# Matmul with rotary embedding on one core: later quarter loads, sixteen block pairs, a split head and a finer last two quads

## The chip, the cores and the metric

The kernel runs on 1 core of one Trainium2 chip. The metric is device time in microseconds (us). Before the change it was 163.15 us, the median of 3 runs (161.26 to 163.74).

## The reference, cut to what matters

```python
batch, seq, hidden, n_heads = (16, 512, 768, 12)      # float32, head_dim = 64
y = np.matmul(x, weight)                              # (16, 512, 768) x (768, 768)
y = y.reshape(batch, seq, n_heads, head_dim)
y1, y2 = y[..., :32], y[..., 32:]
out1 = y1 * cos1 - y2 * sin1                          # cos, sin: (512, 64), the same for all heads
out2 = y2 * cos2 + y1 * sin2
out = np.concatenate([out1, out2], axis=-1).reshape(batch, seq, hidden)
```

## The kernel before, in words

The 8192 rows of x are cut into 64 tiles of 128 rows. Four tiles that use the same rows of cos and sin (the same `r`, four batches) make a quad; there are 16 quads, g = 0 to 15. A tile's products are 12 matmuls: six chunks of 128 of the contracted 768, each in a piece of 512 and one of 256 columns. A quad fills 3072 columns of PSUM, which is six banks of 512 (`py`); two more banks (`pt`) take transposes.

For the product, x has to be cast to fp16 and turned, so that the contracted index lies on partitions. There are two ways:

- **By TensorE.** SyncE loads the tile whole (`load`, L189, 384 KB, rows of 3072 bytes) into one of 10 buffers `xs`. ScalarE casts it (`cast`, L169, `xc<-xs`), TensorE transposes six blocks of 128 x 128 into a PSUM bank (`turn`, L235, `pt<-ident,xc`), and ScalarE copies them back (`xt<-pt`).
- **As a block pair.** Two tiles are loaded together in four quarters (`load_quarter`, L204), each to 32 partitions in pieces of 192 numbers (768 bytes), in such an order that VectorE's transposes of 32 x 32 blocks are all that is left (`turn_pair`, L260, `xp<-xd` or `xp<-xh`). A pair of kind `sp` is loaded by SyncE as fp32 into `xb` (3 buffers) and cast by ScalarE in one instruction (`cast_pair`, `xd<-xb`). A pair of kind `pool` is loaded by GpSimd's queue, which casts to fp16 on the way (`xh<-in_x_dram`); GpSimd spends its own time on issuing these loads. `BLOCKS` names the pairs: the second half (g, 1) of quads 2 to 14, seven of them `sp` and six `pool`. So 26 tiles go by pairs and 38 by TensorE.

After the product, `rope` (L304, L313) takes 1024 columns at a time (a unit, two banks; `units`): VectorE multiplies them from PSUM by cos and by sin in one instruction (`tq<-py,csn`, 2048 results), and GpSimd adds the two halves, one of them with its 32-column halves swapped, into the output buffer (`ov<-tq`). `tq` has three buffers, `ov` four quads. `store` sends 1536 columns of a quad to HBM, from ScalarE's queue, at the first and third tile of the next quad. The last quad has its own units: five of 512 columns, one of 320, and one of 192 in the bank `pt0`, whose add VectorE does.

The order on each engine is written out by hand. `Flow.do` records every instruction with what it reads and writes, and puts the waits in. SyncE first issues the loads `order = [0, "w0", 1, "w1", 2, "w2", 3, "w3", "w4", "w5"]` (x tiles 0 to 3, six chunks of the weight), then cos and sin, and then `fetch`, a list in which x tiles and quarters take turns, as far as buffers are free (`pump`). Quad 0 is computed chunk by chunk as the weight lands (L407 to L442): 12 matmuls on zeros (`warm`), casts of the weight on VectorE (`cast_w`), the products of each chunk (`mm0`). From tile 4 on a loop (L501 to L525) emits, for tile i: its 12 matmuls, the ropes that they complete, the block transposes for tiles up to i + 5 (`B_AHEAD` 6), TensorE's transposes for tile i + 3 (`T_AHEAD` 3), the cast for tile i + 7 (`C_AHEAD` 7), GpSimd's loads for tiles up to i + 19 (`P_AHEAD` 20), and the stores. At the end SyncE waits for all stores (L529), and the program's own closing steps follow (L560: each engine's drain, barriers, a clearing of semaphores). `tile_critical(no_gpsimd_drain=True)` leaves GpSimd's drain out at the end of the hand-written part, so its first one is in the closing steps.

Of the kernel before, what the change touches and what calls it, by code (L numbers as in the profile page):

```python
# [16 lines left out]
class Flow:  # L17
# [23 lines left out]

    def do(self, e, make, reads=(), writes=(), dma=None, tick=True):
        need = {}
        for k in reads:
            for s, v in self.wrote.get(k, {}).items():
                need[s] = max(need.get(s, 0), v)
        for k in writes:
            for d in (self.wrote, self.readby):
                for s, v in d.get(k, {}).items():
                    need[s] = max(need.get(s, 0), v)  # L50
# [53 lines left out]
def kernel(  # L104
# [10 lines left out]
    nc = tc.nc  # L115
# [15 lines left out]
    CHUNKS = [(t, e) for t in range(NT) for e in range(2)]  # L131
    LAST = NG - 1


    BLOCKS = {}
    for g in range(2, 15):
        BLOCKS[g, 1] = "pool" if g % 2 == 0 and g >= 4 else "sp"

    def sbuf(name, shape, dt):
        return nc.alloc_sbuf_tensor(name, shape, dt).ap()  # L140

    NX, NB, NBH, NC, NCP, NXT, NXP, NTQ, NOV = 10, 3, 3, 5, 2, 8, 4, 3, 4

# [6 lines left out]
    xs_b = [sbuf(f"xs{i}", [P, H], FP32) for i in range(NX)]  # L150
    xb_b = [sbuf(f"xb{i}", [P, 2 * H], FP32) for i in range(NB)]
    xh_b = [sbuf(f"xh{i}", [P, 2 * H], FP16) for i in range(NBH)]
# [40 lines left out]
    def load_quarter(gh, q):  # L193
        g, h = gh
        b, r = where(g * QB + 2 * h)
        e = BLOCKS[gh]
        src = x[b : b + 2].rearrange("b (j a r) (q k) -> r q a (b j) k", r=SB, a=R, q=NQ)
        if q == 0:
            xs[gh] = ring("xh", NBH) if e == "pool" else ring("xb", NB)
        k = xs[gh]  # L200
        name = f"xh{k}" if e == "pool" else f"xb{k}"
        buf = xh_b[k] if e == "pool" else xb_b[k]
        dst = buf.rearrange("p (j k) -> p j k", j=2 * NQ)
        do(e, lambda eng: eng.dma_start(out=dst[ts(q, R)], in_=src[r, q]),  # L204
           writes=[f"{name}q{q}"], dma=name)

# [6 lines left out]

    def cast_w(c, e):
        t, h = c
        do(e, copy(e, w_sb[:, t, h], w_raw[:, t, h]),
           reads=[f"wr{t}{h}"], writes=[f"w{t}{h}"])


    def cast(i, e):  # L220
        k = xs[i]
        c = ring("xc", NC)
        xc[i] = c
        do(e, copy(e, xc_b[c].rearrange("p (t m e) -> p t m e", t=NT, e=2),
                   xs_b[k].rearrange("p (m t e) -> p t m e", t=NT, e=2)),
           reads=[f"xs{k}"], writes=[f"xc{c}"])

    def turn(i, e):
        c = xc[i]
        k = ring("pt", 2)  # L230
        z = ring("xt", NXT)
        src = xc_b[c].rearrange("p (t m e) -> p t e m", t=NT, e=2)
        pt = pt_b[k].bitcast(FP16)[:, 0:H].rearrange("p (t e m) -> p t e m", t=NT, e=2)
        for t, h in CHUNKS:
            do("pe", lambda eng: eng.transpose(pt[:, t, h, :], src[:, t, h, :], ident),  # L235
               reads=[f"xc{c}", "ident"], writes=[f"pt{k}"], tick=(t, h) == CHUNKS[-1])
        do(e, copy(e, xt_b[z], pt), reads=[f"pt{k}"], writes=[f"xt{z}"])
        xT[i] = (lambda t, h: xt_b[z][:, t, h, :], f"xt{z}")

# [8 lines left out]
    def turn_pair(gh):  # L248
# [12 lines left out]
        for s in (0, 1):  # L261
            xT[g * QB + 2 * h + s] = (
                lambda t, e, s=s: v[:, t, e, ts(s, P)], f"xp{z}")

    def units(g):
        if g < LAST:
            return [(c, c + 1024, py[:, c : c + 1024], [f"ps{c // 512}", f"ps{c // 512 + 1}"], "pool")
                    for c in (0, 1024, 2048)]  # L270
        u = [(c, c + 512, py[:, c : c + 512], [f"ps{c // 512}"], "pool") for c in range(0, 2560, 512)]
        u.append((2560, 2880, py[:, 2560:2880], ["ps5"], "pool"))
        u.append((2880, 3072, pt_b[0][:, 0:192], ["pt0"], "dve"))
        return u

    def pieces(g, s):

        out_, lo = [], s * H
        for c0, c1, ps, banks, _ in units(g):
            step = 512 if len(banks) > 1 else c1 - c0  # L280
            for k, b in enumerate(banks):
                a, z = max(lo, c0 + k * step), min(lo + H, c0 + (k + 1) * step)
                if a < z:
                    out_.append((a, z, ps[:, a - c0 : z - c0], b))
        return out_

    def mm_piece(i, piece, c, start, stop, tick):
        g, s = divmod(i, QB)
        a, z, ps, bank = piece
        get, key = xT[i]  # L290
        t, h = c
        do("pe", lambda eng: eng.matmul(  # L292
            ps, get(t, h), w_sb[:, t, h, a - s * H : z - s * H], start=start, stop=stop),
            reads=[key, f"w{t}{h}"], writes=[bank], tick=tick)

    ov_of = {}

    def rope(g, u):
        c0, c1, ps, banks, adder = u
        w, r = c1 - c0, g % SB  # L300
        k = ring("tq", NTQ)
        nh = w // D
        tq = tq_b[k][:, :, 0:w]
        do("dve", lambda eng: eng.tensor_tensor(  # L304
            out=tq.rearrange("p j (h d) -> p j h d", d=D),
            in0=ps.rearrange("p (h d) -> p h d", d=D)
            .unsqueeze(1).broadcast_to((P, 2, nh, D)),
            in1=csn[:, :, r, :].unsqueeze(2).broadcast_to((P, 2, nh, D)),
            op=MULT), reads=banks + ["csn"], writes=[f"tq{k}"])
        if g not in ov_of:  # L310
            ov_of[g] = ring("ov", NOV)
        o = ov_of[g]
        do(adder, lambda eng: eng.tensor_tensor(  # L313
            out=ov_b[o][:, ds(c0, w)].rearrange("p (h t d) -> p h t d", t=2, d=HD),
            in0=tq[:, 0].rearrange("p (h t d) -> p h t d", t=2, d=HD),
            in1=tq[:, 1].rearrange("p (h t d) -> p h t d", t=2, d=HD)[:, :, ::-1, :],
            op=ADD), reads=[f"tq{k}"], writes=[f"ov{o}c{c}" for c in range(c0, c1, 64)])

# [19 lines left out]

    order = [0, "w0", 1, "w1", 2, "w2", 3, "w3", "w4", "w5"]
    for k in order:  # L340
# [9 lines left out]

    fetch, quarters = [], []
    soon = [p for p in sorted(BLOCKS) if BLOCKS[p] == "sp"]
    for i in range(QB, NTILE):
        if soon and i >= (soon[0][0] - 1) * QB:
            quarters += [(soon[0], q) for q in (0, 2, 1, 3)]
            soon.pop(0)
        if not is_block(i):
            fetch.append(i)
            if quarters:
                fetch.append(quarters.pop(0))  # L360
        elif quarters and quarters[0][0] == pair_of(i):
            fetch.append(quarters.pop(0))
    fetched = [0]
    xs_used, xb_used = [0], [0]
    xs_sent, xb_sent = [4], [0]

# [35 lines left out]

    def castx(i, e):
        cast(i, e)
        xs_used[0] += 1

    U0 = units(0)  # L407
    warm(9)
    castx(0, "dve")
    cast_w(CHUNKS[0], "dve")  # L410
    turn(0, "dve")
    castx(1, "act")
    warm(3)
    mm0(0, CHUNKS[0])
    cast_w(CHUNKS[1], "dve")
    turn(1, "act")
    mm0(0, CHUNKS[1])
    mm0(1, CHUNKS[0])
    mm0(1, CHUNKS[1])
    castx(2, "act")  # L420
    cast_w(CHUNKS[2], "dve")
    turn(2, "act")
    for i in (0, 1):
        mm0(i, CHUNKS[2])
    castx(3, "act")
    for c in CHUNKS[:3]:
        mm0(2, c)
    turn(3, "act")
    cast_w(CHUNKS[3], "dve")
    for i in (0, 1, 2):  # L430
        mm0(i, CHUNKS[3])
    for c in CHUNKS[:4]:
        mm0(3, c)
    cast_w(CHUNKS[4], "dve")
    for i in range(4):
        mm0(i, CHUNKS[4])
    cast_w(CHUNKS[5], "dve")
    do("dve", lambda eng: eng.tensor_copy(
# [3 lines left out]
        reads=["sin", "csn1", "cos"], writes=["csn"])  # L442
    assert not quarters
    pump()

    state = {"cast": 4, "turn": 4, "bturn": 0, "pool": 0}
    pairs = sorted(BLOCKS)
    pool_pairs = [p for p in pairs if BLOCKS[p] == "pool"]

    def casts(upto):  # L450
        while state["cast"] < min(upto, NTILE):
            i = state["cast"]
            state["cast"] += 1
            if not is_block(i):
                castx(i, "act")
            elif i % 2 == 0 and BLOCKS[pair_of(i)] == "sp":
                cast_pair(pair_of(i))
                xb_used[0] += 1
            pump()

    def turns(upto):
        while state["turn"] < min(upto, NTILE):
            i = state["turn"]
            state["turn"] += 1
            if not is_block(i):
                turn(i, "act")

# [16 lines left out]

    C_AHEAD, T_AHEAD, B_AHEAD, P_AHEAD = 7, 3, 6, 20


    for i in range(4):
        mm0(i, CHUNKS[5])
        if i == 1:  # L490
            casts(6)
            turns(5)
            rope(0, U0[0])
    casts(7)
    turns(6)
    rope(0, U0[1])
    rope(0, U0[2])
    casts(8)
    turns(7)

    for i in range(QB, NTILE):  # L501
# [12 lines left out]
        turns(i + 1 + T_AHEAD)  # L514
        casts(i + 1 + C_AHEAD)
        pool_loads(i + P_AHEAD)
# [9 lines left out]
    store(LAST, 2 * H, 3 * H, "sp")  # L526
    store(LAST, 3 * H, 2880, "act")
    store(LAST, 2880, 4 * H, "sp")
    f.finish("sp", [f"ov{o}c{c}" for o in range(NOV) for c in range(0, QB * H, 64)])  # L529
# [35 lines left out]
```

## Time and profile before

| | |
|---|---|
| median of 3 runs | 163.15 us (161.26, 163.15, 163.74) |
| the profiled execution | 162.36 us, span 160.6 us |
| busy share | PE 91%, DVE 80%, POOL 79%, ACT 45% |
| mean granted TensorE clock | 0.974 |
| DMA | 50.77 MB, mean 316 GB/s |
| HBM | 27.79 MB read, 25.17 MB written |

PE is TensorE's matmuls, PEld its weight loads, DVE is VectorE, ACT ScalarE, POOL GpSimd, SP SyncE; a q behind a name is the engine's sequencer, which waits, branches and issues DMAs. L292 is line 292 of the kernel. A group row gives the line, the engine, the operation, what is written and read, the count, then the busy time and the mean of one in ns, and behind the bar the idle time of the engine just before, with what ended it. The chain of waits is followed back from the last instruction: at each step to what released it. Times in a timeline are from the span's start. The span is what the profiler saw on the core; the device time of the same execution is 1.8 us more.

### The profile page before, as it was taken

What the parts mean: (1) busy time and instruction counts of PE and PEld (TensorE: products, weight loads), DVE (VectorE), ACT (ScalarE), POOL (GpSimd) and SP (SyncE); (2) the same over time, 40 slices, a digit from 0 to 9 for tenths busy, and PEclk for the clock granted to TensorE, in tenths of its full rate; (3) what the DMA queues carried; (4) which work ended last, traced back from release to release, by engine and by line L of the source; (5) the groups of instructions that cost most, each with busy time, mean ns of one, the idle gap of its engine ahead of it and who ended that gap; (6) DMA issues with size and microseconds to landing.
All of it is one profiled execution on the core that took longest, in us unless ns stands there. A gap on an engine that the chain in (4) does not pass through costs nothing.

```text
span 160.6 us, 2527 instructions
## 1 busy us (share of the span) xinstructions
PE 145.8 (91%) x1014; PEld 90.0 (56%) x1014; DVE 128.1 (80%) x77; ACT 72.2 (45%) x82; POOL 127.2 (79%) x81
## 2 busy tenths in 40 slices
PE   6889569999999999999999999999999999999600
PEld 2336336656565666666666666665656566666500
DVE  0624783499999799989999899897989899789830
ACT  3272466895234653454354527461655247131000
POOL 1000299749999999999999998999989797988950
PEclk9999987999999999999999999999999999999985
DMA  4999999999999999999999999999999975555860
GB/s 107 409 406 319 259 265 278 275 330 356 347 335 354 367 396 280 353 382 400 296 351 388 410 302 354 377 411 316 351 372 404 416 299 196 196 196 205 329 248 7
DMA packets 29660, 50.77 MB, mean 316 GB/s; under 512 B 8272, under 2 KB 15824, under 8 KB 29648
## 3 DMA queue, kind: packets, MB, share of 16 engines
q1 hardware_dynamic: 14672, 23.96, 46.8%
q10 hardware_dynamic: 8448, 24.28, 38.1%
q0 software_dynamic: 6528, 2.36, 11.9%
q8 instruction: 8, 0.13, 0.3%
q14 instruction: 4, 0.03, 0.0%
HBM read 27.79 MB, written 25.17 MB: 330 GB/s over the span
## 4 chain that ended last, share of the span: by engine, by line
PE 76%; DMA 7%; SPq 5%; POOL 4%; issue 2%; DVE 1%; ACT 1%; DVEq 0%
PE py L292 69%; DMA xs<-in_x_dram 7%; PE pt L235 7%; POOL ov L313 4%; SPq L211 2%; SPq L189 2%; DVE tq L304 1%; SPq L204 1%; ACT xc L169 1%; SPq L345 0%; SPq L347 0%; SPq L560 0%; DVEq L55 0%; SPq L114 0%
## 5 line engine op out<-in xcount | busy, mean ns | idle before, releaser
L313 POOL TENSOR_TENSOR ov<-tq 128x1024 f32<-128x1024 f32 (+2 forms) x51 | 112.8, 2237 | 26.7 <-DVE tq L304 26.1
L304 DVE TENSOR_TENSOR tq<-py,csn 128x2048 f32<-128x2048 f32 (+2 forms) x51 | 108.7, 2146 | 12.9 <-PE py L292 12.5
L292 PE MATMUL py<-w_sb,xt 128*128 128x256 f16 (+1 forms) x456 | 79.2, 329 | 0.5 <-ACT xt L169 0.2
L292 PEld LDWEIGHTS py<-w_sb,xt 128*128 128x128 f16 x456 | 44.3, 99 | 30.5 <-ACT xt L169 1.4
L292 PE MATMUL py<-w_sb,xp 128*128 128x256 f16 (+1 forms) x312 | 54.9, 326 | 0.0
L169 ACT COPY xt<-pt 128x768 f16<-128x768 f16 x37 | 29.5, 798 | 39.3 <-PE pt L235 32.6
L169 ACT CAST xc<-xs 128x768 f16<-128x768 f32 x37 | 33.2, 902 | 23.4 <-DMA xs<-in_x_dram 23.3
L292 PEld LDWEIGHTS py<-w_sb,xp 128*128 128x128 f16 x312 | 29.4, 98 | 16.8
L235 PE MATMUL pt<-ident,xc 128*128 128x128 f16 x228 | 19.3, 222 | 3.5 <-ACT xc L169 3.0
L235 PEld LDWEIGHTS pt<-ident,xc 128*128 128x128 f16 x228 | 15.7, 99 | 10.2 <-ACT xc L169 4.9
L169 ACT CAST xd<-xb 128x1536 f16<-128x1536 f32 x7 | 11.3, 1617 | 10.4 <-DMA xb<-in_x_dram 10.4
L204 POOL DMA_DIRECT2D xh<-in_x_dram x24 | 14.0, 590 | 0.0
L260 DVE STREAM_TRANSPOSE xp<-xd 128x768 f32<-128x768 f32 x7 | 6.8, 971 | 3.2 <-ACT xd L169 3.2
L260 DVE STREAM_TRANSPOSE xp<-xh 128x768 f32<-128x768 f32 x6 | 7.5, 1243 | 0.0
L169 DVE CAST w_sb<-w_raw 128x768 f16<-128x768 f32 x6 | 3.4, 560 | 4.4 <-DMA w_raw<-in_weight_dram 4.4
L390 PE MATMUL py<-cold 128*128 128x512 f16 x12 | 4.8, 568 | 1.4 <-DVE cold L333 1.4
L169 DVE CAST xc<-xs 128x768 f16<-128x768 f32 x1 | 1.0, 953 | 3.4 <-DMA xs<-in_x_dram 3.4
L390 PEld LDWEIGHTS py<-cold 128*128 128x128 f16 x12 | 1.4, 132 | 3.4 <-issue 1.9
L169 ACT ACT_TABLE_LOAD x1 | 1.3, 1283 | 0.9 <-SPq L114 0.9
L333 DVE MEMSET cold<- 128x256 uint32 x1 | 0.3, 272 | 1.1 <-SPq L114 1.1
L304 DVE TENSOR_TENSOR tq<-pt,csn 128x384 f32<-128x384 f32 x1 | 0.6, 558 | 0.4 <-POOL ov L313 0.4
L313 DVE TENSOR_TENSOR ov<-tq 128x192 f32<-128x192 f32 x1 | 0.8, 812 | 0.0
(11 smaller groups left out, 3.1 us busy)
## 6 DMA issues: line engine op xcount, KB each, us to landing
out_dram<-ov ACTq DMA_DIRECT2D x30, 768.0 KB, 8.4
xs<-in_x_dram SPq DMA_DIRECT2D x38, 384.0 KB, 17.5
xb<-in_x_dram SPq DMA_DIRECT2D x28, 192.0 KB, 17.0
w_raw<-in_weight_dram SPq DMA_DIRECT2D x6, 384.0 KB, 6.8
xh<-in_x_dram POOLq DMA_DIRECT2D x24, 96.0 KB, 11.7
out_dram<-ov SPq DMA_DIRECT2D x2, 384.0 KB, 2.5
out_dram<-ov ACTq DMA_DIRECT2D x1, 384.0 KB, 2.7
out_dram<-ov ACTq DMA_DIRECT2D x1, 288.0 KB, 2.5
```

The source lines that it names most:

```text
L169: eng.copy(out=o, in_=i_) if e == "act" else eng.tensor_copy(out=o, in_=i_)
L189: do(e, lambda eng: eng.dma_start(out=xs_b[k], in_=x[b].rearrange("(p r) h -> r p h", r=SB)[r]), writes=[f"xs{k}"], dma=f"xs{k}")
L204: do(e, lambda eng: eng.dma_start(out=dst[ts(q, R)], in_=src[r, q]), writes=[f"{name}q{q}"], dma=name)
L211: do(e, lambda eng: eng.dma_start(out=w_raw[:, t, h], in_=wv[t, h]), writes=[f"wr{t}{h}"], dma=f"w{t}{h}")
L235: do("pe", lambda eng: eng.transpose(pt[:, t, h, :], src[:, t, h, :], ident), reads=[f"xc{c}", "ident"], writes=[f"pt{k}"], tick=(t, h) == ...
L260: do("dve", lambda eng: eng.transpose(out=dst, in_=src), reads=rd, writes=[f"xp{z}"])
L292: do("pe", lambda eng: eng.matmul(ps, get(t, h), w_sb[:, t, h, a - s * H : z - s * H], start=start, stop=stop), reads=[key, f"w{t}{h}"], w ...
L304: do("dve", lambda eng: eng.tensor_tensor(out=tq.rearrange("p j (h d) -> p j h d", d=D), in0=ps.rearrange("p (h d) -> p h d", d=D) .unsque ...
L313: do(adder, lambda eng: eng.tensor_tensor(out=ov_b[o][:, ds(c0, w)].rearrange("p (h t d) -> p h t d", t=2, d=HD), in0=tq[:, 0].rearrange(" ...
L333: do("dve", lambda eng: eng.memset(cold, 0.0), writes=["cold"])
L390: do("pe", lambda eng: eng.matmul(py[:, ts(b, 512)], cold[:, 0:P], cold, start=True, stop=warmed[0] < WARM - 6), reads=["cold"], writes=[f ...
```

## The change

The instructions that compute the result stay the same in kind; what changes is which tiles go which way, when they are loaded, and how the first quad and the last two are cut.

- **Pairs.** There are 16 block pairs in place of 13: (g, 1) of quads 4 to 14 and (g, 0) of quads 6, 8, 10, 12, 14; four of them ((4, 1), (6, 1), (8, 1), (10, 1)) are loaded by GpSimd, twelve by SyncE. 32 tiles go by pairs and 32 by TensorE. The first pair is in quad 4, where it was in quad 2.
- **Loads.** The quarters of a pair whose first tile is n stand in SyncE's queue behind tiles n - 8, n - 6, n - 4 and n - 2, so the queue now begins with x tiles 5 to 14 and no quarter among them. There are 12 buffers `xs` (10) and 4 `xb` (3), three of which lie in the fp32 weight, once that is cast (`after=` adds the wait).
- **Head.** x tile 4 is loaded ahead of the last chunk of the weight. The casts and the copies back of tiles 0 to 3 are shared: a third (256 columns) on VectorE, two thirds (512) on ScalarE. Tile 4 is cast and turned before the last chunk's products.
- **Loop.** Pair casts have an own place (`pair_casts`, 7 tiles ahead); block transposes are emitted 4 tiles ahead in place of 6; the single casts' lead grows from 4 to 7 over the first tiles.
- **End.** The last two quads are cut by banks of 512 (the last: five of 512, one of 256 and one of 256 in `pt0`). For the unit in `pt0` VectorE does two multiplications of 256 and the add, whose first operand is now in PSUM. GpSimd gets a drain of its own behind its last add.

The core of the diff:

```diff
-    BLOCKS = {}
-    for g in range(2, 15):
-        BLOCKS[g, 1] = "pool" if g % 2 == 0 and g >= 4 else "sp"
+    BLOCKS = {(g, 1): "sp" for g in range(4, 15)}
+    BLOCKS.update({(g, 0): "sp" for g in (6, 8, 10, 12, 14)})
+    BLOCKS.update({(g, 1): "pool" for g in (4, 6, 8, 10)})
...
-    NX, NB, NBH, NC, NCP, NXT, NXP, NTQ, NOV = 10, 3, 3, 5, 2, 8, 4, 3, 4
+    NX, NB, NBH, NC, NCP, NXT, NXP, NTQ, NOV = 12, 4, 3, 5, 2, 8, 4, 3, 4
...
-    xb_b = [sbuf(f"xb{i}", [P, 2 * H], FP32) for i in range(NB)]
+    xb_b = [w_raw.rearrange("p t e n -> p (t e n)")[:, ts(i, 2 * H)] for i in range(NT)]
+    xb_b += [sbuf(f"xb{i}", [P, 2 * H], FP32) for i in range(NT, NB)]
...
-        if g < LAST:
+        if g < LAST - 1:
             return [(c, c + 1024, py[:, c : c + 1024], [f"ps{c // 512}", f"ps{c // 512 + 1}"], "pool")
                     for c in (0, 1024, 2048)]
-        u = [(c, c + 512, py[:, c : c + 512], [f"ps{c // 512}"], "pool") for c in range(0, 2560, 512)]
-        u.append((2560, 2880, py[:, 2560:2880], ["ps5"], "pool"))
-        u.append((2880, 3072, pt_b[0][:, 0:192], ["pt0"], "dve"))
+        u = [(c, c + 512, py[:, c : c + 512], [f"ps{c // 512}"], "pool") for c in range(0, 3072, 512)]
+        if g == LAST:
+            u[-1] = (2560, 2816, py[:, 2560:2816], ["ps5"], "pool")
+            u.append((2816, 3072, pt_b[0][:, 0:256], ["pt0"], "dve"))
...
+        if adder == "dve":
+            for dst, j, wr in ((tq[:, 1].rearrange("p (h d) -> p h d", d=D), 1, keys), (ph, 0, banks)):
+                do("dve", lambda eng: eng.tensor_tensor(
+                    out=dst, in0=ph, op=MULT,
+                    in1=csn[:, j, r, :].unsqueeze(1).broadcast_to((P, nh, D))),
+                    reads=banks + ["csn"], writes=wr)
+            do("dve", lambda eng: eng.tensor_tensor(
+                out=o, in0=ps.rearrange("p (h t d) -> p h t d", t=2, d=HD),
+                in1=swapped, op=ADD), reads=keys + banks, writes=okeys)
+            return
...
-    order = [0, "w0", 1, "w1", 2, "w2", 3, "w3", "w4", "w5"]
+    order = [0, "w0", 1, 2, "w1", 3, "w2", "w3", "w4", 4, "w5"]
...
+    fetch = [(i, i) for i in range(QB + 1, NTILE) if not is_block(i)]
+    for gh in BLOCKS:
+        if BLOCKS[gh] == "sp":
+            n = gh[0] * QB + 2 * gh[1]
+            fetch += [(n - 8 + 2 * k + 0.5, (gh, q)) for k, q in enumerate((0, 2, 1, 3))]
+    fetch = [j for _, j in sorted(fetch, key=lambda v: v[0])]
...
+    BOTH = (("dve", 0, 1), ("act", 1, NT))
     U0 = units(0)
-    warm(9)
-    castx(0, "dve")
+    warm(10)
+    castx(0, *BOTH)
+    turn(0, *BOTH)
...
+    castx(4, ("act", 0, NT))
+    cast_w(CHUNKS[4], "dve")
+    for i in range(4):
+        mm0(i, CHUNKS[4])
+    turn(4, ("act", 0, NT))
+    cast_w(CHUNKS[5], "dve")
...
-    C_AHEAD, T_AHEAD, B_AHEAD, P_AHEAD = 7, 3, 6, 20
+    C_AHEAD, T_AHEAD, PC_AHEAD, B_AHEAD, P_AHEAD = 7, 3, 7, 4, 20
...
-        casts(i + 1 + C_AHEAD)
+        casts(i + 1 + min(C_AHEAD, QB + (i - QB) // 2))
+        pair_casts(i + PC_AHEAD)
...
     store(LAST, 2 * H, 3 * H, "sp")
-    store(LAST, 3 * H, 2880, "act")
-    store(LAST, 2880, 4 * H, "sp")
+    nc.gpsimd.drain()
+    store(LAST, 3 * H, 2816, "act")
+    store(LAST, 2816, 4 * H, "sp")
```

## The prediction

> **What bounds the kernel now.** I read the page's busy shares first, then the chain of waits in order of time, then the timeline of head, one middle stretch and tail, and last the closing steps. The chain says where the end is set:
>
> ```profile
> 8.94 11.55 DMA xs<-in_x_dram
> 20.51 0.91 ACT xc L169
> 21.46 0.51 PE pt L235 x6
> 21.97 3.21 PE py L292 x12
> ...
> 140.78 1.96 PE py L292 x12
> 142.75 0.03 issue
> ...
> 142.84 2.30 DVE tq L304
> ...
> 151.23 3.43 POOL ov L313 x3
> ```
>
> Columns: start, duration, what. Three stages: up to 21.8 us x tiles 5 and 6 are late, from there to 142.78 TensorE never waits, and from 142.78 VectorE and GpSimd finish quads 14 and 15. The reader is to see that TensorE's work between the first and the second mark is a plain sum: 56 tiles (4 to 59) at 5.85/3 = 1.95 us (chain rows of 36 matmuls) are 109.3, the transposes of the 29 tiles from 7 to 61 that go by TensorE at 0.335 are 9.7, and 1.7 is a slow clock: 120.7, against 121.0 seen. The clock stands in the table of stretches (busy us and instructions of PE, PEld, DVE, ACT, POOL, then the granted clock, the DMA share and GB/s):
>
> ```profile
> 15.66:19.07 3.41, 2.31 (x19) 1.31 (x16) 2.19 (x1) 1.23 (x2) 0.00 (x0) 1.00 1.03 241
> 19.07:22.49 3.42, 1.54 (x16) 1.01 (x17) 3.42 (x3) 2.82 (x4) 3.23 (x2) 1.00 1.11 254
> 22.49:25.90 3.41, 3.41 (x18) 2.11 (x17) 1.08 (x1) 1.63 (x3) 3.41 (x2) 0.50 1.02 282
> ```
>
> A stretch in which TensorE was busy 1.54 of 3.42 us is followed by one at half clock: 3.41 us of work cost 1.7 more. VectorE is close behind TensorE; its timeline in the middle gives the spacing from start to start:
>
> ```profile
> 77.69 2.29 DVE L304 TENSOR_TENSOR tq<-py,csn 128x2048 f32<-128x2048 f32 x1 [0.31 <-PE py L292]
> 79.89 1.24 DVE L260 STREAM_TRANSPOSE xp<-xh 128x768 f32<-128x768 f32 x1
> 81.07 2.24 DVE L304 TENSOR_TENSOR tq<-py,csn 128x2048 f32<-128x2048 f32 x1
> ...
> 86.16 2.29 DVE L304 TENSOR_TENSOR tq<-py,csn 128x2048 f32<-128x2048 f32 x1 [0.31 <-PE py L292]
> 88.36 0.97 DVE L260 STREAM_TRANSPOSE xp<-xd 128x768 f32<-128x768 f32 x1
> 89.25 2.25 DVE L304 TENSOR_TENSOR tq<-py,csn 128x2048 f32<-128x2048 f32 x1
> ```
>
> So a unit takes 2.20, a block transpose 1.18 (`xh`) or 0.89 (`xd`). The tail is GpSimd's, seven adds without a gap, and the close is a drain (its row: min/median/max in ns, then first and last start):
>
> ```profile
> 145.21 9.45 POOL L313 TENSOR_TENSOR ov<-tq 128x1024 f32<-128x1024 f32 x7 [0.51 <-DVE tq L304]
> ```
> ```profile
> L560 POOLq DRAIN  x3: 45/129/2019, 157.6 to 160.3; - x3
> ```
>
> **The change, part by part.** All terms are against the profiled execution (162.36 us, span 160.6), which lies 0.8 under the median of 163.15.
>
> Head. In the timeline the loads of 384 KB land 0.97 us apart (x0's cast starts at 4.76, x1's at 6.68, the last weight chunk's at 13.61). x4 now lies ahead of that chunk, which comes at 14.6, so its cast ends at 15.1 and the four tiles' last products (8 pieces, 4 x 0.335) end at 17 at the soonest; the first unit started at 16.88 and starts at about 16.7: nothing moves there. What moves is x5 and x6. Before, three quarters lay among them and they landed at 18.7 and 20.5; with none, x5 lands 1.6 behind the last chunk (cos and sin 0.6, itself 0.97), at 16.2. Then ScalarE and TensorE set the pace: T4 ends at 15.9 (behind the fifth chunk's products), copy 0.80, cast of x5 0.89, transposes 0.4, copy 0.80, cast of x6 0.89, transposes 0.4: tile 4's products start at 20.1 in place of 21.8, **-1.7**. Ends: -2.6 if T4 runs 0.9 earlier, 0 if the loads stay late. The shared casts (two thirds of ScalarE's 902 ns, a third of VectorE's 953) lie beside TensorE's backlog of 20 chunk products and cost nothing; were it gone, two VectorE pieces of about 0.3 a tile would show.
>
> Clock. On the same grid of 3.41 us TensorE would be busy 1.9 (15.66 to 19.07) and 2.7 (to 22.49). 2.31 kept the clock, 1.54 lost it. 1.9 lies between, 2.7 above both; I take no drop, **-1.7**; other end 0. The Trainium skill ("TensorE: Matmul & The Clock Gate", Why this matters for your kernels) says that an idle gap of about 3 us brings the clock down. Here the gaps ahead of the drop were 1.68 and 1.30 us, so by that rule the drop is not the gap's work, the change need not take it away, and the sum would be 1.7 higher. The row decides.
>
> Transposes. Six tiles fewer go by TensorE in the middle (23 for 29): 6 x 0.335 = **-2.0**, if VectorE keeps up. An even and an odd quad from 6 to 11 take TensorE 8 x 1.95 + 2 x 0.335 = 16.3 us; VectorE 6 x 2.20 + 2 x 0.89 + 1.18 = 16.2 (15.9 where all three pairs are `sp`). It fits by 0.1 us. The block transpose now stands directly ahead of its use: for (g, 1) it follows the quad's last unit, so 2.20 + 1.24 of VectorE must fit in the two tiles (3.9 us) ahead of it. Ends: -2.0, and 0 if VectorE paces it (rival B). GpSimd needs 6 x 2.33 for the adds and 2.31 for four loads, 16.3, but its four loads stand by quads 0, 1, 3 and 5 and it only lags some 3 us there; with three `tq` buffers VectorE feels a lag above 8.1 - 2.29 - 2.37 = 3.4. ScalarE loses six casts and copies and gains five pair casts of 1.62; it waits 39 us for TensorE now. The stores that stand in its queue wait for GpSimd's lag of 3 us, and what is behind them, the copies, is due three tiles (5.9 us) later.
>
> Loads. Six whole tiles go, five `sp` pairs come, two `pool` pairs go. By the queue rows ACT's stores take 38.1% of 160.6 us for 24.28 MB, 2.5 us a MB, so a whole tile 1.0; the six `pool` pairs 11.9%, 3.2 each; what is left of SyncE's 46.8% is at most 4.1 for an `sp` pair, at least 2.0 if its bytes cost as a tile's. That is between -2.4 and +8 us of DMA work over 130 us in which the engines were full. I take 3.0 (+2.6). Hidden: all loads are in at 130 us now, and the last is turned at 145; SyncE may run 10 to 16 tiles (20 to 32 us) ahead with four `xb`, against 17 us to landing. The wait added for the weight's casts was over at 14 us. The Trainium skill ("DMA: Bandwidth & Descriptors", Specifications) asks for 512 bytes and more a piece; by it 768 bytes are at full rate, an `sp` pair costs two tiles, and the loads would shrink by 2.4; the row of `pool` pairs speaks against it.
>
> Tail. From tile 59's end (E) TensorE still needs 8.44. GpSimd now: quad 13's last add ends 4.7 behind quad 14's start, which is E - 8.5; eleven adds of 512 at the spacing seen in the tail, (9.45 - 2.37 - 0.98)/5 = 1.22, are 13.4, one of 256 0.9: E + 10.5; with waits between the last ones E + 10.7. Before it was 154.66 - 142.78 = 11.9: **-1.2**. Ends: -1.9 (TensorE's 8.44, one multiplication, one add), 0 if GpSimd enters quad 14 late by 1.2. VectorE alone: free at E + 9.1, two multiplications of 0.42 (from 384 results in 0.56 and 1024 in 1.22), an add between 0.42 and 0.81 (the row of 192): E + 10.4 to 10.8, level with GpSimd. Six adds for three in quad 14 cost 0.5 more (1.275 x 6 - 2.371 x 3), inside this count.
>
> Drain. The last store lands at 157.2, and the first drain of the close takes 2.02 us behind it; the second and third, with nothing in between, 0.05 and 0.13. The own drain runs behind GpSimd's last add, beside the store's 2.5 us to landing, and the closing one should be short: **-1.9**. Ends: -2.0, and 0 if the drain at the close costs the same whatever went before.
>
> Sum: -1.7 - 1.7 - 2.0 - 1.2 - 1.9 = -8.5; 162.36 - 8.5 = 153.9. Against the median it would be 154.7; I take 154.3.
>
> **The rivals.**
>
> B: VectorE paces quads 6 to 13. For it: by durations (2.278, 0.971, 1.243) in place of spacings two quads take 16.85, not 16.3. Against it: rows that follow each other overlap by 0.06. Price: 3 x 0.57 + 0.3 = 2.0: **156.3**.
>
> C: two terms fail, the drain (+1.9) and the clock (+1.7): the change does not do what it says there. For it: 1.9 us busy is under the 2.31 that is known to be safe. **157.9**.
>
> D: DMA gives out moderately. At 4.1 a pair, two middle quads need 2.0 + 8.2 + 3.2 + 7.9 = 21.3 of packet time, and the stretches carry at most 1.18 of it: 18.0 us, 1.7 over TensorE, some 8 us to quad 14, of which the lead takes half: **158.5**.
>
> E, the other side: DMA starves. With quarters and no stores (22 to 27 us) only 264 GB/s were moved. Two quads move 6.3 MB; at 264 GB/s 23.9 us, 7.6 over TensorE, over 4.5 such pairs 34, less a lead of 12: **176**. It turns slower than before below about 300 GB/s. Against it: where both kinds are in flight the stretches show 313 (92 to 97 us) to 388 (72 to 77 us).
>
> **How the numbers follow.** Forecast 0.56, own range 152.5 to 156; B 0.18; C 0.12; D 0.07; E 0.05; about no change 0.02. All good ends together are -10.2, 152.2, and the lowest of the runs is 1.1 under the profiled one: low 151.5. High 159.5 takes in B, C and D. About 2% can be told from no change, 159.9 to 166.4: faster 0.9, same 0.04, slower 0.06.
>
> **What would show it.** Right: tile 4's first matmul near 20.1; granted clock 1.0 from 5 to 145 us; tile 59 ending near 137.4; 10.7 us from there to GpSimd's last add; first closing drain near 0.1 us. Wrong: VectorE without idle time in quads 6 to 13 and TensorE waiting for `xp` or for `tq`'s reads of `py` (B); a half clock near 20 us, a closing drain of 2 us (C); ScalarE waiting for `w_raw` or `xb` loads and TensorE behind it (D, E).

## The result, and the profile after

| | before | after |
|---|---|---|
| median of 20 runs each | 162.88 us (161.26 to 165.43) | 165.56 us (163.79 to 170.94) |
| ratio to before | | 1.0126, 95% interval 1.0091 to 1.0162 |
| profiled execution, its span | 162.36, 160.6 us | 170.94, 169.2 us |
| TensorE's last matmul ends | 151.22 us | 161.95 us |
| last landing of a store to the end of the span | 3.4 us | 1.7 us |

The kernel became 1.3% slower; 154.3 us had been forecast, in a range of 151.5 to 159.5. The ratio is of undisturbed runs alone, so it is not quite that of the medians, and the profiled execution of after happens to be the slowest of its runs; a second profile of the same kernel, at 164.26 us (span 162.5), shows the same waits, and the sizes below are taken from it where that is said.

The chain of waits of after (start, duration, what), where the chain of before had nothing but TensorE between 22 and 142.8 us:

```profile
31.79 1.95 PE py L307 x12
34.92 18.60 DMA xs<-in_x_dram
...
57.38 1.50 ACT xd L172
59.26 6.77 SPq L207
...
75.46 15.80 DMA xs<-in_x_dram
91.29 0.89 ACT xc L172
92.73 1.97 PE py L307 x12
...
114.10 1.63 ACT xd L172
116.14 1.55 SPq L207
...
121.84 10.23 DMA xs<-in_x_dram
132.10 0.90 ACT xc L172
133.05 0.82 PE pt L246 x6
```

The reader sees three loads of a single x tile that take 10 to 19 us each, and behind each of them ScalarE's cast, twice with TensorE's transposes right after it. Such a load is not slower than before the change (from issue to landing a tile takes 12.1 us at the median, 17.5 before): it is issued too late. `SPq L207` is SyncE issuing a quarter: the issue itself takes up to 6.8 us, because the queue is full (the run m1 below shows this alone). The waits of ScalarE say the same (us in total, times, longest); after first, then its second profile, then before:

```profile
ACT xc L172 <- DMA xs<-in_x_dram: 54.0, 10, 10.9
...
ACT xd L172 <- DMA xb<-in_x_dram: 1.3, 1, 1.3
```
```profile
ACT xc L172 <- DMA xs<-in_x_dram: 45.2, 12, 7.8
```
```profile
ACT xc L169 <- DMA xs<-in_x_dram: 23.3, 15, 4.5
...
ACT xd L169 <- DMA xb<-in_x_dram: 10.4, 6, 2.2
```

It is the whole tiles that come late, not the quarters that were added. What hangs on such a late tile is seen in ScalarE's timeline of after (start, duration, then the instruction; ACTq issues DMAs):

```profile
91.29 0.88 ACT L172 CAST xc<-xs 128x768 f16<-128x768 f32 x1 [3.17 <-DMA xs<-in_x_dram]
91.30 0.90 ACTq L363 DMA_DIRECT2D out_dram<-ov  x2
...
92.78 0.55 ACTq L363 DMA_DIRECT2D out_dram<-ov  x1
...
94.91 0.38 ACTq L363 DMA_DIRECT2D out_dram<-ov  x1
```

The tile issued at 75.46 is in at 91.26, and in the same moment two stores go out, and two more within 3.6 us. Three of the four had been ready, the first for 10.5 us (its last add ended at 80.85); they stood behind the cast in ScalarE's queue. The fourth waited for its own add. SyncE is held up too. A quarter may be issued when its buffer `xb` is free, the pair cast that frees it stands behind the late tile's cast, and the next tiles stand behind the quarter in SyncE's queue: from 85.70 to 93.70 SyncE issued nothing, and the chain above goes this way twice (`ACT xd`, then `SPq L207`). Its waits of this kind, after, then before, when it waited rather for tile buffers (25.3 us) with its loads far enough ahead:

```profile
SPq L207 <- ACT xd L172: 19.5, 5, 8.0
```
```profile
SPq L204 <- ACT xt L169: 1.9, 2, 1.0
SPq L204 <- ACT xc L169: 1.3, 2, 0.9
```

Meanwhile the transfers moved little, though the DMA engines were busy (share 0.97). The table of stretches of after (busy us and instructions of PE, PEld, DVE, ACT, POOL, then granted clock, DMA share, GB/s):

```profile
17.07:20.49 3.42, 1.35 (x12) 0.64 (x10) 3.34 (x2) 2.76 (x4) 0.97 (x1) 1.00 1.03 399
20.49:23.90 3.41, 3.41 (x14) 1.70 (x15) 3.34 (x2) 1.59 (x2) 3.41 (x2) 0.50 1.03 399
```
```profile
87.00:92.00 5.00, 2.46 (x18) 1.43 (x18) 3.51 (x2) 1.60 (x2) 3.26 (x2) 1.00 0.97 188
92.00:97.00 5.00, 4.78 (x35) 3.12 (x36) 2.58 (x2) 4.57 (x5) 2.36 (x1) 1.00 0.99 377
```

From 87.9 us, when the last store had landed, to 91.3 only quarters and one tile were in flight. The stretch around it moved 188 GB/s; once the stores are let out, 377. The first two lines are the head: the stretch ahead of tile 4's products is busy 1.35 us and the next one runs at half clock, as before the change. VectorE in the middle keeps the forecast spacing: from one `xh` transpose to the next, two quads, 85.19 - 68.84 = 16.35 us (forecast 16.2 for VectorE, 16.3 for TensorE).

```profile
68.84 1.25 DVE L272 STREAM_TRANSPOSE xp<-xh 128x768 f32<-128x768 f32 x1
...
85.19 1.23 DVE L272 STREAM_TRANSPOSE xp<-xh 128x768 f32<-128x768 f32 x1
```

The closing drains of after (min/median/max ns, first and last start), 2019 ns at most before:

```profile
L596 POOLq DRAIN  x3: 39/47/128, 167.9 to 168.9; - x3
```

### The profile page after: what moved, and what is told of

Its sections match the earlier page's. It is cut to its first block, busy times and chain, and to the rows that moved or that the text cites. A ratio compares the mean times of both kernels' runs of the same rounds, so it can differ in the third digit from the quotient of the medians.

```text
span 169.2 us, 2478 instructions
## 1 busy us (share of the span) xinstructions
PE 147.3 (87%) x978; PEld 89.4 (53%) x978; DVE 129.3 (76%) x90; ACT 68.7 (41%) x77; POOL 122.8 (73%) x76
## 3 DMA queue, kind: packets, MB, share of 16 engines
q0 software_dynamic: 4352, 1.57, 7.5%
## 4 chain that ended last, share of the span: by engine, by line
DMA 26%; PE 20%; SPq 13%; DVE 12%; POOL 10%; ACT 10%; issue 5%; POOLq 1%; ACTq 0%; DVEq 0%
DMA xs<-in_x_dram 26%; PE py L307 13%; SPq L207 11%; DVE tq L344 10%; POOL ov L349 10%; PE pt L246 4%; ACT xd L172 4%; ACT xt L172 3%; ACT xc L172 3%; PE py L418 3%; DVE xp L272 2%; SPq L192 2%; POOLq L562 1%; ACTq L363 0%; DVE xt L172 0%
## 5 line engine op out<-in xcount | busy, mean ns | idle before, releaser
L307 PE MATMUL py<-w_sb,xp 128*128 128x512 f16 (+1 forms) x384 | 67.6, 334 | 0.0
L307 PE MATMUL py<-w_sb,xt 128*128 128x256 f16 (+1 forms) x384 | 67.1, 329 | 0.2 <-DVE xt L172 0.2
L307 PEld LDWEIGHTS py<-w_sb,xp 128*128 128x128 f16 x384 | 37.9, 100 | 24.7 <-issue 1.6
L172 ACT CAST xc<-xs 128x768 f16<-128x768 f32 (+1 forms) x32 | 27.2, 868 | 57.1 <-DMA xs<-in_x_dram 54.0
L307 PEld LDWEIGHTS py<-w_sb,xt 128*128 128x128 f16 x384 | 37.0, 99 | 23.9 <-issue 2.2
L172 ACT COPY xt<-pt 128x768 f16<-128x768 f16 (+1 forms) x32 | 24.3, 773 | 24.3 <-PE pt L246 24.3
L172 ACT CAST xd<-w_raw 128x1536 f16<-128x1536 f32 x9 | 14.5, 1608 | 1.4 <-DVE xp L272 1.4
L272 DVE STREAM_TRANSPOSE xp<-xd 128x768 f32<-128x768 f32 x12 | 11.5, 962 | 0.0
L207 POOL DMA_DIRECT2D xh<-in_x_dram x16 | 9.3, 590 | 0.0
L172 ACT CAST xd<-xb 128x1536 f16<-128x1536 f32 x3 | 4.9, 1623 | 4.5 <-DVE xp L272 3.2
## 6 DMA issues: line engine op xcount, KB each, us to landing
xs<-in_x_dram SPq DMA_DIRECT2D x32, 384.0 KB, 12.1
```

The source lines that it names most:

```text
L172: eng.copy(out=o, in_=i_) if e == "act" else eng.tensor_copy(out=o, in_=i_)
L272: do("dve", lambda eng: eng.transpose(out=dst, in_=src), reads=rd, writes=[f"xp{z}"])
L307: do("pe", lambda eng: eng.matmul(ps, get(t, h), w_sb[:, t, h, a - s * H : z - s * H], start=start, stop=stop), reads=[key(t)] + wkeys(c, ...
```

## The experiments

Two theories of the lost time were set against each other. The **order theory** (Q): a whole tile stands in SyncE's queue behind quarters that are needed later, its cast holds up ScalarE, and ScalarE holds up the stores, so that the queues run empty of stores and then overfull. The **work theory** (W): five more fp32 pairs are more than the queues carry, in whatever order. Times are medians of all runs; ratios are to the kernel before on the same chip, with 95% intervals.

| kernel | pairs (GpSimd's) | order | us (before) | ratio |
|---|---|---|---|---|
| after | 16 (4) | after's | 165.56 (162.88) | 1.013 [1.009, 1.016] |
| e1_casts_late | 16 (4) | after's | 163.99 (164.95) | 0.993 [0.987, 1.000] |
| e2_tiles_first | 16 (4) | tiles first | 160.30 (164.95) | 0.969 [0.958, 0.980] |
| e3_both | 16 (4) | tiles first, casts late | 164.43 (164.95) | none given |
| e6_six_pool | 16 (6) | tiles first | 159.47 (163.05) | 0.971 [0.957, 0.984] |
| e10_half_way | 16 (6) | tiles 4 ahead | 159.24 (164.71) | 0.964 [0.955, 0.974] |
| e9_14_pairs | 14 (6) | tiles first | 157.93 (164.71) | **0.959 [0.950, 0.967]** |
| e11_14_after_order | 14 (6) | after's | 161.20 (164.10) | 0.982 by the medians, no interval |
| e7_13_pairs | 13 (6) | after's | 161.26 (163.05) | 0.988 [0.977, 0.999] |
| e8_13_first | 13 (6) | tiles first | 167.61 (164.71) | 1.017 [1.009, 1.025] |
| e13_13_lead | 13 (6) | mended head | 161.54 (163.80) | 0.997 [0.991, 1.003] |
| e4_before_drain | before's | before's | 161.80 (163.05) | 0.994 [0.989, 0.999] |
| e5_before_tail | before's | before's | 160.72 (164.95) | 0.978 [0.969, 0.987] |

**What a load costs (m1_dma_prices).** Transfers of this kernel's shapes, with nothing computed: 48 quarters alone, 12 stores alone, both together, tiles alone, tiles and stores.

```diff
+    quarters_(halves_[:12], 1, [])            # SyncE
+    stores_(halves_[:12], 2, t1)              # ScalarE
+    quarters_(halves_[12:24], 3, t2); stores_(halves_[12:24], 3, t2)
+    tiles_(halves_[:12], t3)
```

> Computes nothing: four stretches of transfers alone, each begun when the one before has landed. 48 quarters (12 pairs) alone; 12 stores of 768 KB alone; 48 quarters and 12 stores together; 24 whole tiles alone; then 24 tiles and 8 stores. By the prediction a pair is 2.0 to 4.1 us of DMA time and the sum of kinds counts: 48 quarters alone 36 us (3.0 a pair), the stores 23.6, together 60, tiles 24. Theory Q says that quarters alone cannot fill DMA: 12 pairs alone 45 to 52 us (3.8 to 4.3 a pair), and together with the stores only 52 to 60, so that the stores come nearly free beside quarters.

Its table of stretches; only the last column counts: quarters alone, stores alone, both at once, quarters left over:

```profile
10.00:40.00 30.00, 0.00 (x0) 0.00 (x0) 1.00 1.11 232
48.00:68.00 20.00, 0.00 (x0) 0.00 (x0) 1.00 1.03 395
72.00:100.00 28.00, 0.00 (x0) 0.00 (x0) 1.00 1.05 404
104.00:130.00 26.00, 0.00 (x0) 0.00 (x0) 1.00 1.12 234
```

A pair takes 3.4 us alone (0.85 a quarter, 232 GB/s); a store 2.0; a tile 0.98. The 48 quarters alone took 43.5 us (36 by the prediction, 45 to 52 by theory Q), and with the 12 stores 63.0 (60; 52 to 60): the stores do not come free. Side by side, the 12 stores moved in 29.2 us (72.2 to 101.4), and in that time only 12 quarters: 2.43 us for each of both. A quarter and a store have 256 packets each, of 768 and 3072 bytes. One packet of the one goes with one of the other, so the quarters get a fifth of 404 GB/s, 81, and a pair beside stores takes 9.7 us. That fits the Trainium skill ("DMA: Bandwidth & Descriptors", Queues, rings and completion order), by which a DMA engine serves its queues in turn, a packet from each. Tiles, whose packets are as long as the stores', got about half: 14 tiles in 28.4 us beside eight stores, 2.0 us a tile. Whether 232 GB/s comes of the 768 bytes or of the 32 partitions that a quarter fills is not separated here.

By these prices two quads with three pairs by SyncE, as 12 and 13 of after, need, as an estimate, four stores with four quarters (4 x 2.43), eight quarters more (8 x 0.85) and two tiles (2 x 0.98): 18.5 us, against TensorE's 16.3. So there the loads fall behind by 2 us in two quads even when something is always in flight. In quads 6 to 11 one pair in three is GpSimd's, which was not priced alone.

**Order.** First the casts later, then the tiles earlier, then both.

```diff
-    C_AHEAD, T_AHEAD, PC_AHEAD, B_AHEAD, P_AHEAD = 7, 3, 7, 4, 20     # e1, e3
+    C_AHEAD, T_AHEAD, PC_AHEAD, B_AHEAD, P_AHEAD = 4, 3, 7, 4, 20
-    fetch = [(i, i) for i in ...]                                     # e2, e3
+    fetch = [(i - 8 if i >= 16 else i - 11, i) for i in ...]
```

> The changed kernel with the casts of single tiles emitted at most 4 tiles ahead (C_AHEAD 4 in place of 7), nothing else. Theory Q (queue): in ScalarE's queue the cast of a single tile, 8 tiles ahead of its use, waits for a load that stands behind quarters in SyncE's queue; the stores and pair casts behind it stand still, and quarters without stores beside them move at 190 to 230 GB/s. Emitted later, the cast finds its load landed: ScalarE's wait for xs falls from 54 us to under 20, TensorE's wait for xc (13 us) to under 6, time 155 to 160 us. Rival W (work): the packets of twelve fp32 pairs are more than DMA can carry in the time, wherever the casts stand: 163 to 167 us, the waits move to other instructions.

> The changed kernel with each single tile's load 8 places further ahead in SyncE's queue, so that it stands ahead of the quarters that are cast after it, nothing else. Theory Q: the early casts find their loads, the stores flow, ScalarE's wait for xs falls under 20 us, 155 to 160 us. Rival W: the bytes and packets are the same, so 163 to 167 us, with ScalarE now waiting for quarters (xd) as long as it waited for xs.

> Both: single casts at most 4 tiles ahead and single tiles' loads 8 places earlier. Theory Q: as good as the better of the two alone or up to 2 us better, 154 to 159 us. Rival W: 163 to 167 us.

Later casts alone take the waits for tiles from 54.0 us (45.2 in the second profile) to 31.4, and four gaps of TensorE of 0.6 to 2.2 us stay; the time is what the work theory gave. Tiles first takes 4.4 points off the ratio. The waits of e2:

```profile
ACT xd L172 <- DMA w_raw<-in_x_dram: 20.1, 6, 7.2
...
ACT xd L172 <- DMA xb<-in_x_dram: 7.0, 2, 5.4
ACT xc L172 <- DMA xs<-in_x_dram: 5.2, 3, 2.0
```

The wait for tiles is nearly gone, and TensorE has no gap over 0.2 us from 21 to 124 us, where one of 2.02 us comes; but 27 us of waiting for quarters have come in its place. So the order was most of the loss, and the load is near its limit all the same. Both edits together are not settled: the four runs took 159.2, 164.2, 164.7 and 164.9 us. In the profile of the one at 164.7 TensorE waits 4.57 us for a cast up to 126 us; whether the run at 159.2 has this gap is not known.

**Work.** Two pairs back to GpSimd (e6), two pairs fewer on top (e9), the tiles only four places ahead (e10), and e9's pairs in the order of after (e11).

```diff
-    BLOCKS.update({(g, 0): "sp" for g in (6, 8, 10, 12, 14)})
+    BLOCKS.update({(g, 0): "sp" for g in (6, 10, 14)})                  # e9, e11
-    BLOCKS.update({(g, 1): "pool" for g in (4, 6, 8, 10)})
+    BLOCKS.update({(g, 1): "pool" for g in (4, 6, 8, 10, 12, 14)})      # all four
+    fetch = [(i - 4 if i >= 16 else i - 11, i) for i in ...]            # e10; e6, e9: i - 8
```

> Single tiles first (as e2), and the pairs (12, 1) and (14, 1) go back to GpSimd's queue: ten fp32 pairs and six pool pairs, 16 as in the change. Theory L (load queue): what is left of the stall in e2, at 126 us, is SyncE's quarters of quads 12 to 14, three fp32 pairs in a row on one queue; with a second queue carrying a third of them the stall goes, 157 to 159 us, ratio 0.955 to 0.965 and no TensorE gap above 0.5 us behind 25 us. Rival G: GpSimd's eight more loads (4.6 us of its time) land where it is already near its limit, 160 us or more.

> Tiles first, six pairs by GpSimd, and two of the five even pairs, (8, 0) and (12, 0), back to single tiles: 14 pairs, eight by SyncE. Work theory: a pair by SyncE takes 3.4 us of the queues alone and up to 9.7 beside stores, against 2.0 for two tiles, so two fewer in the quads where they stand three in two quads free at least 2.8 us; ScalarE's waits for quarters fall from 46 us (ten pairs) to under 25, the four gaps of TensorE (3.9 us in all) go, TensorE gets four transposed tiles more (1.3 us): ratio 0.955 to 0.965. Order theory alone: the waits stay as they are, and the ratio is 0.97 to 0.98.

> Sixteen pairs, six by GpSimd, as in the run of six, with single tiles four places ahead of the quarters in SyncE's queue in place of eight. Order theory: somewhere between none and eight lies an order without either wait; ScalarE's waits for tiles and quarters together fall from 46 us to under 20 and the ratio is 0.955 to 0.965. Work theory: what one kind of load gains the other loses; the waits together stay at 35 to 55 us, TensorE keeps 3 to 5 us of gaps, and the ratio is 0.968 to 0.98.

> Fourteen pairs, six by GpSimd, eight by SyncE, as in the run at 0.959, but SyncE's queue in the order of the changed kernel. Work theory (the quarters that were added are what costs time, wherever they stand): ratio 0.955 to 0.97, ScalarE's wait for tiles under 25 us. Order theory (a whole tile behind quarters makes ScalarE late, and stores with it): ScalarE's wait for tiles stays at 35 us or more, TensorE has gaps over 0.8 us between 85 and 135 us, and the ratio is 0.98 to 1.0. Between the two, both count.

Two pairs more by GpSimd changed nothing that can be measured, and the gaps that theory L saw go are still four, of 0.9 to 1.1 us. Two pairs fewer gave the lowest ratio of all, 6.8 us under before, though its interval overlaps those of e2, e6 and e10; its waits for quarters fell less than the work theory had said (46 to 31 us), but only one gap of TensorE is left, 0.80 us, and the clock stays at 1.0 until the last matmul. The chain of e9 has one late load in place of three:

```profile
85.76 18.96 DMA w_raw<-in_x_dram
106.30 0.82 ACT xt L172
107.26 4.06 PE py L307 x24
```

Half way (e10) is the same as e6 within the intervals: tiles and quarters together wait 39 us (11.2 and 27.8; in e6 50), as the work theory said, while the ratio is as the order theory said. It decides nothing. In e11 fourteen pairs in the order of after wait 27.8 us for tiles (45.2 in the second profile of after), between what the two theories said, with gaps of 0.3, 0.4 and 1.45 us only.

```profile
ACT xc L172 <- DMA xs<-in_x_dram: 27.8, 10, 6.0
```

Its ratio is loose: the seven runs of before lie from 161.6 to 167.1 us there, and against the two shortest (161.6 and 161.9) e11's 161.2 is 0.996. So from after to e11 (four pairs fewer by SyncE) the ratio falls by 1.6 to 3 points, from e11 to e9 (order) by 2.3 to 3.8. Clear of the intervals are two steps: from after to e2 (order alone, at sixteen pairs) 4.4 points, and from after to e7 below (five pairs fewer by SyncE, two more by GpSimd, in after's order) 2.5. Both theories count; whether the order is dearer the more quarters there are is not shown.

**Thirteen pairs.** The pairs of before with the rest of the change (e7), then tiles first (e8), then two tries to get the first pair in earlier.

```diff
+    BLOCKS = {(g, 1): "sp" for g in range(2, 15)}                       # e7, e8, e12, e13
+    BLOCKS.update({(g, 1): "pool" for g in (4, 6, 8, 10, 12, 14)})
+    fetch = [(i - 8 if i >= 16 else i - 11, i) for i in ...]            # e8
+    fetch = [(i - 8 if i >= 16 else i - 4, i) for i in ...]             # e12
+    fetch = [(max(i - 8, 9) if i >= 16 else i - 11 if i < 9 else 9, i) for i in ...]  # e13
```

> The changed kernel with the 13 pairs of before (seven fp32, six pool; 38 tiles by TensorE) and everything else of the change, its load order too. If the three extra pairs and the two moved to SyncE bring the stalls: ScalarE's wait for xs falls from 54 us under 30, TensorE has no gap above 1 us behind 25 us, and the time is 2.0 us over a stall-free 16-pair version, 157 to 160. If the load order or the casts' place in ScalarE's queue does it with any pairs: 162 to 166.

> The thirteen pairs of the kernel before, the rest of the change, and the single tiles ahead of the quarters in SyncE's queue. Only four kinds of gain are left: head (0.7), tail (0.7 to 1.2), drain (1.7 to 1.9), and no wait in the middle. Order theory: with thirteen pairs the late tiles were all that cost time, so ScalarE's wait for tiles falls from 38.7 us to under 8, TensorE has no gap behind 23 us, and the ratio to before is 0.975 to 0.982. Work theory: seven pairs by SyncE are within what the queues carry, so here too nothing starves: 0.975 to 0.982; both theories fail if the waits for quarters rise above 15 us.

> Thirteen pairs, tiles first from tile 16 on, but tiles 5 to 13 only four places ahead of the first two pairs' quarters, so that the pair that was cast at 32.66 us is in earlier. If that one late cast was all of it, the gap of 7.9 us at 35.7 us and the 10.2 us of half clock behind it go, TensorE has no gap over 0.5 us behind 25 us, and the time falls from 167.6 by 7.9 and up to 5.1 us to 155 to 160 (ratio 0.94 to 0.97). If the waits only move, a gap of 2 us or more stands elsewhere and the ratio is over 0.98.

> Thirteen pairs, tiles first from tile 16 on; in the head tiles 5 to 8, then the first pair's four quarters among six, then tiles 9, 12 and 13. Six quarters at 0.85 to 1 us behind tile 8 (landed at 20) have the first pair in at 25 in place of 32.6 us, when its cast is due. If that late cast was all, no gap of TensorE over 1 us and no half clock stands behind 25 us, and the time is 155 to 160, ratio 0.94 to 0.97. If the quarters and tiles of the head are too much for the queue whatever their order, a wait of over 4 us of ScalarE for tile 9, 12 or 13 takes its place, with a gap of TensorE of 3 us or more before 45 us, and the ratio is over 0.98.

In e7 ScalarE waits 38.7 us for tiles, but never over 4.1 at once, and TensorE has no gap over 0.45 us behind 23 us: without the five added pairs by SyncE the order of after does no harm in the middle. It costs in the head, where quarters lie among the first tiles again: tile 4's products start at 22.9 us, in after at 21.1. Tiles first, expected at 0.975 to 0.982, came out at 1.017, from one wait. ScalarE's timeline of e8:

```profile
32.66 1.55 ACT L171 CAST xd<-w_raw 128x1536 f16<-128x1536 f32 x1 [7.39 <-DMA w_raw<-in_x_dram]
32.67 0.43 ACTq L362 DMA_DIRECT2D out_dram<-ov  x1
34.12 0.79 ACT L171 COPY xt<-pt 128x768 f16<-128x768 f16 x1
```

The first pair belongs to quad 2, and with all early tiles ahead of it its quarters land at 32.6 us. The copy of a tile stands behind its cast; TensorE waits 7.86 us, and 10.24 us are at half clock (30.8 to 41.0). Neither theory had this. In e12 the list put tile 16's load ahead of tile 13's while the buffers are freed in the order of tiles, so a buffer was filled again before the cast of its tile, which stood for 16.75 us behind that later load; its output is wrong, and its 185 us say nothing about the question. In e13 the first pair is in at 27 us, but the second now is late (its cast at 41.69 waits 8.62 us), with gaps of 2.35 and 3.05 us: the wait only moved. So with the tiles put first, the pairs of quads 2 and 3 come late; in e7 and before, where their quarters lie among the tiles, they do not. An order that serves both the head and thirteen pairs was not found.

**The tail and the drain alone.** Both on the kernel before.

```diff
+    nc.gpsimd.drain()                                # e4: this alone; e5: with the new units
-        if g < LAST:                                 # e5: units, pieces and rope as in after
+        if g < LAST - 1:
```

> The kernel before with GpSimd's own drain alone. By the prediction's term: 1.9 us less than before (ratio 0.988), first closing drain near 0.1 us in place of 2.0. Rival: the drain's time only moves, ratio 1.00.

> The kernel before with only the end changed: last two quads by banks, VectorE's unit of 256 with its add from PSUM, GpSimd's own drain. By the prediction's two terms (-1.2 tail, -1.9 drain): 159.8 us, closing drain near 0.1 us. Rival: the drain costs its 2 us wherever it stands or the finer adds eat the gain, 161.5 to 163.

The drain gives 1.0 us (interval 0.2 to 1.9), half of what the term said and more than the rival's nothing; in e4's trace the close shrinks from 3.4 to 1.7 us, with this row of closing drains:

```profile
L561 POOLq DRAIN  x3: 39/47/129, 158.5 to 159.5; - x3
```

Tail and drain together give 3.6 us (2.2 to 5.0). In e5's trace the last add ends 2.77 us behind TensorE's last matmul, against 3.44 before.

**The changed kernel once more (a0).**

> The changed kernel once more, for a second profile: the first was of its slowest execution (170.94 us against a median of 165.56). Order and work theories alike: the same waits, ScalarE 40 to 55 us for whole-tile loads, TensorE with gaps of 0.8 to 3 us between 85 and 135 us. If the half clock at 130 us (6.8 us of it, so about 3.4 us lost) is a matter of where the grid of 3.41 us falls, it is shorter or absent here and the span is 163 to 166.

Timeline of TensorE in this second profile:

```profile
107.28 0.51 PE L246 MATMUL pt<-ident,xc 128*128 128x128 f16 x6 [1.94 <-ACT xc L172]
...
123.48 0.51 PE L246 MATMUL pt<-ident,xc 128*128 128x128 f16 x6 [2.03 <-ACT xc L172]
```

The span is 162.5 us. The wait for tiles is 45.2 us, the gaps are 1.94, 2.03 and 0.44 us, and the half clock in the middle is 3.4 us long, not 6.8. The half clock follows the gap at 123 us, not that at 107.

## Why the prediction was wrong, step by step

The second profile's 164.26 us stand against the sum's 153.9. TensorE's last matmul ends at 155.25; the sum had tile 59 at 137.4 and 8.44 us to it, 145.8. Of the 9.4 us between, gaps are 4.4 (three), the half clock in the head that did not go 1.7, a second half clock behind a gap 1.7, the head 0.9; 0.7 are not assigned. The tail adds 0.6 and the close 0.4.

- **Loads: the step that failed.** "Hidden: all loads are in at 130 us now" and "SyncE may run 10 to 16 tiles (20 to 32 us) ahead". The price was nearly right (3.0 a pair taken, 3.4 measured alone); hiding it was not. Four things were left out: whole tiles stand behind quarters in one queue; the queue of quarters gets 81 GB/s beside stores and not a share by need; a late cast stops the stores, without which the engines move 188 to 232 GB/s in place of 400; and it stops SyncE, whose next quarter waits for the buffer of a pair cast behind it (19.5 us in after, 14.6 in its second profile). The lead was counted in tiles allowed by buffers, while the full queue set it. The sign that was named for it, ScalarE waiting for `w_raw` or `xb`, did not come in after: ScalarE waited for `xs`. That order and number of pairs cost the time is shown by e2 and e7; how much of it goes through the stores and how much through the held-up buffers is not separated, as no run has more `xb` buffers or stores from another engine.
- **The row set against full rate for 768 bytes does not bear on it.** The `pool` pairs' packets hold 384 bytes (2.36 MB in 6528 packets). What m1 shows is 232 GB/s for packets of 768.
- **Rival E was put aside by a stretch of before.** "Where both kinds are in flight the stretches show 313 ... to 388." True of after as well (377 at 92 us), but that both kinds are in flight is what broke. E's own mechanism, quarters without stores, appears in pieces (188 GB/s at 87 to 92 us, 220 at 107 to 112), between D's 158.5 us and E's 176. The two had 0.12 together.
- **Head: right in kind, mis-sized.** x5 landed at 16.2 us in the one profile, as forecast, and at 17.1 in the other, but the copy of tile 4 began at 16.6 and 16.8 in place of 15.9, as its transposes stand behind the fifth chunk's products. Tile 4's first product came at 21.0 (20.1 forecast, 21.8 before): -0.8 for -1.7.
- **Clock: failed as a forecast.** The stretch held 1.35 to 1.55 us of work, not the 1.9 of the sum, and half clock followed. The sum also kept before's grid, and the grid starts elsewhere in each execution, so which way this term goes is partly luck. The runs show that the criterion was nearly the right one: 1.73 in e9 kept the clock.
- **Transposes, VectorE: right.** Two quads take 16.3 us, so rival B did not happen.
- **Tail: about half.** From TensorE's last matmul to the last add 2.8 us, for 2.26 forecast and 3.44 before.
- **Drain: right in the close** (-1.7 for -1.9); of the time of the whole kernel e4 shows 1.0. The own drain itself took 3.5 us in after, from 162.6 on, beside the last adds and the last store's way to HBM.

The terms outside the middle do pay where the middle runs: e9's span is 4.2 us under that of before in their two profiles, of which TensorE's last matmul is 2.0, the tail 0.7 and the close 1.7, less 0.2 for the last store. The low end of the range, 151.5, does not follow from its working (152.2 less 1.1 is 151.1); nothing hangs on it.

## What to carry to other kernels

A load that is "hidden" has to be followed through its queue: which load stands behind it, which instruction of which engine waits for that one, and what else stands behind that instruction, stores and the freeing of load buffers above all. Two queues that share the DMA engines divide them by packets, so short packets beside long ones lose out, and a price from a quiet stretch is too low by nearly three (3.4 us and 9.7 us for the same pair). Where a stage is near its limit, try one addition less and the order of need before giving the idea up: the same change with two pairs fewer, two more by GpSimd and the tiles first took 4.1% off.

## What the runs showed of the hardware that had not been expected

**The clock goes by fixed stretches.** In sixteen profiled executions (about 700 stretches of 3.41 us, each on the grid that its clock record shows) every stretch at full clock with 1.41 us or less of TensorE's work was followed by half clock (12 of 12 ahead of TensorE's last tiles), none with 1.57 us or more was, and of five between 1.50 and 1.55 three were. Where the grid falls differs from one execution to the next, so the same gap of 1.7 us in the head cost 1.7 us in some and nothing in others; a gap of 3.05 us, split by the grid, cost no clock in e13, and one of 2.03 us did in the second profile of after:

```profile
120.69:124.11 3.42, 1.39 (x12) 0.66 (x11) 2.82 (x2) 0.89 (x1) 2.85 (x3) 1.00 1.10 226
124.11:127.52 3.41, 3.41 (x12) 1.40 (x10) 1.09 (x1) 0.42 (x1) 1.90 (x1) 0.50 1.12 211
```

The Trainium skill ("TensorE: Matmul & The Clock Gate", Part 1: The HAM clock gate) has the free-running window of 3413 ns, and these runs agree; it has the clock fall after an idle window, where here a window 40% busy was enough.

**A full queue blocks the engine that issues.** In m1, where SyncE had nothing else to wait for, issuing a quarter took 0.45 us at the median for the first 13; from then on some nine quarters were unfinished at any time, and an issue took 0.76 us, about as long as a quarter's transfer (0.85). Beside stores it took 1.7 us. In after it took up to 6.8 us (`SPq L207` in the chain), so where loads stand in the program and when they start are two things.
